# Holding four small products back until both of their loads are in, in a two-layer decoder trunk

## The chip, the cores and the metric

The kernel runs on one core of one Trainium2 chip. The metric is the device time of one execution in microseconds (us), as the median of several runs. All profiles are of that one core.

## The reference, cut to what matters

Two layers, each with two sub-layers, on 256 tokens of 1024 features. Six vectors of 1024 features per layer (shift, scale and gate of each sub-layer) come from one small vector `c` and a large matrix:

```python
c_act = jax.nn.silu(c)                                    # [1, 1024]
for l in range(DEPTH):                                    # 2
    ada = c_act @ w_ada[l] + b_ada[l]                     # [1, 1024] @ [1024, 6144]
    sh1, sc1, gt1, sh2, sc2, gt2 = split(ada, 6)
    u = x * (1.0 + sc1) + sh1
    y = mixer(u, ...)             # one wide projection; attention; convolution of 31 taps; two gates; output
    x = layer_norm(ALPHA * x + (1.0 + gt1) * y, ...)
    u = x * (1.0 + sc2) + sh2
    h = square(relu(u @ w_up[l])) @ w_down[l]
    x = layer_norm(ALPHA * x + (1.0 + gt2) * h, ...)
```

The change touches `sh2` and `sc2` of layer 0 alone: two thousand columns of `w_ada[0]`, each a dot product over 1024 features. They are needed when `u` of the second sub-layer is made.

## The kernel before, in words

All large weights stream through the core once, in units of 128 x 1024 (512 KB). `Stream.make` (lines 109 to 127) loads a unit on the queue of the SP engine (L118), copies its high part on ScalarE (`wh`, L121) and subtracts to get the low part on VectorE (`wl`, L122). Five raw tiles and eight split tiles are there, so up to eight units stand split ahead of the products. Each product is made of three matmuls of parts (L314 to L316 with 512 columns, L320 to L322 with 256).

Work that isn't weight products is traced in steps between the units by the class `Background`: the convolution (`conv_steps`, on VectorE and ScalarE), the attention (`attn_steps`), and the second shift and scale of layer 0, `ada_pe_cols(0, 4)` and then `ada_pe_cols(0, 3)`. A scheduler then orders each engine's instructions: among those that its own estimate of time calls ready, the one traced earliest goes first. After that every engine works through its own list strictly in that order, and so does the SP queue, which issues both the weight loads (L118) and the loads of `w_ada` (L379). A wait at the head of a list holds all that stands behind it.

Two thousand columns are four chunks of 512. For a chunk, `ada_pe_chunk` makes four loads of 256 x 512 (512 KB, two row blocks of 128 each) into tiles `ada`, of which there are three. After the second and after the fourth load, `ada_part` (L385) issues four products: each has a stationary operand of 32 columns (one of them with values) and writes its own 32 rows of one bank `adab`, side by side in the array (`tile_position=(0, 32 * j)`). Two of the four read the first load's tile and two the second's. After eight products ScalarE copies the bank (`adae`, L394), TensorE transposes it (`adat`, L368), and VectorE adds the four rows up (`adac`, L422, L423). So there are 16 loads and 8 groups of four products. A float32 product is two matmul records in the profile, so a group is 8 records and one half of it, a pair, is 4.

The first shift and scale go through the same `ada_part`, called from `ada_pe`, which the change leaves as it is (`adabs` in the profile).

Of the kernel before, what the change touches and what calls it, by code (L numbers as in the profile page):

```python
# [69 lines left out]
class Background:  # L70
    """Work that is traced a step at a time between the weight units; each step says after how many
    units the next one comes."""
# [18 lines left out]
    def finish(self, gen, until=None):  # L91
        """the rest of gen, or its steps until a condition holds"""
        for e in list(self.gens):
            if e[0] is gen and until is None:
                self.gens.remove(e)
        while until is None or not until():
            if next(gen, self) is self:
                break


class Stream:
    """The weights in the order of their use: each unit of [128, 1024] is loaded once and
    split exactly into a high and a low part, ahead of the products that take it."""
# [47 lines left out]
def trunk_kernel(ctx: ExitStack, tc: tile.TileContext, x_in, c_in, positions, w_in, w_attn_br,  # L151
                 conv_dw_w, conv_dw_b, conv_ln_g, conv_ln_b, w_conv_pw, w_out, w_ada, b_ada,
                 ln_mix_g, ln_mix_b, w_up, w_down, ln_ffn_g, ln_ffn_b, out):
    nc = tc.nc
# [48 lines left out]
    def load_ada0(k0, nk):  # L203
        """128 nk columns each of the first shift and scale"""
        src = w_ada[0, :, 0:2 * D].rearrange("(j p) (v n) -> p j v n", p=128, v=2)
        r = []
        for q in range(2):
            p, tag = (c_p, "c") if k0 % 2 else (g_p, "g")
            t = p.tile([128, 4, 2, 128 * nk], F32, name=f"ada0_{k0}{q}", tag=tag)
            for v in range(2):  # L210
                nc.sync.dma_start(t[:, :, v, :], src[:, 4 * q:4 * q + 4, v, 128 * k0:128 * (k0 + nk)])
                if small:
                    next(small[0], None)
            r.append(t)
        return r

    small = []
# [4 lines left out]
    rows, taps = [], []  # L222
    posi = const.tile([128, 2], I32, name="posi")

    def vector_loads(l):
        """per-feature vectors as rows, a load at a time"""
        r = t_p.tile([92, 128], F32, name=f"rows{l}", tag="t")
        rows.append(r)
        t = t_p.tile([4 * CK, 128], F32, name=f"taps{l}", tag="t")
        taps.append(t)  # L230
        o = 0
        for v, n in ((b_ada, 48), (ln_mix_g, 8), (ln_mix_b, 8), (ln_ffn_g, 8), (ln_ffn_b, 8),
                     (conv_ln_g, 4), (conv_ln_b, 4), (conv_dw_b, 4)):
            nc.sync.dma_start(r[o:o + n, :], v[l:l + 1, :].rearrange("o (j p) -> (o j) p", p=128))
            o += n
            yield
        nc.sync.dma_start(t, conv_dw_w[l].rearrange("j (q p) -> (j q) p", p=128))
        yield
        if l == 0:
            for h in range(2):  # L240
                nc.sync.dma_start(posi[:, h:h + 1], positions[0:1, H[h]].rearrange("o p -> p o"))
                yield
# [25 lines left out]
    units = []  # L268
# [35 lines left out]
    def order(later, earlier):  # L304
        """on the same engine, with no wait"""
        tc.add_manual_dep(later.ins, earlier.ins.name,
                          mybir.DependencyInfo(mybir.DependencyClass.NoSync, mybir.DependencyReason.DATA), reason="order")
# [4 lines left out]
    def rowmm(b, lh, ll, wh, wl, first, last):  # L312
        """b[tok, n] += lhs^T w, from the parts."""
        nc.tensor.matmul(b, lh, wh, start=first, stop=False, skip_group_check=True)  # L314
        nc.tensor.matmul(b, lh, wl, start=False, stop=False, skip_group_check=True)  # L315
        return nc.tensor.matmul(b, ll, wh, start=False, stop=last, skip_group_check=True)  # L316

    def colmm(b, wh, wl, rh, rl, first, last):
        """b[feat, tok] += w^T rhs, from the parts; two groups share a bank."""
        nc.tensor.matmul(b, wh, rh, start=first, stop=False, skip_group_check=True)  # L320
        nc.tensor.matmul(b, wh, rl, start=False, stop=False, skip_group_check=True)  # L321
        nc.tensor.matmul(b, wl, rh, start=False, stop=last, skip_group_check=True)  # L322

    def place(instrs, n):
        """instrs, of TensorE, after the next n products of a unit's half that are traced"""
        places.append([n, instrs])
# [21 lines left out]
    def col_group(ids, rhs, banks):  # L348
        """banks: two of [128, 2 feature tiles x 256]; units of [128, 2 kt, 512]."""
        for n, i in enumerate(ids):  # L350
            wh, wl = ws.live[i]
            for k in range(2):
                rh, rl = rhs(2 * n + k)
                first, last = n == 0 and k == 0, n == len(ids) - 1 and k == 1
                for f in range(4):
                    fs = slice(512 * k + 128 * f, 512 * k + 128 * f + 128)
                    o = banks[f // 2][:, 256 * (f % 2):256 * (f % 2) + 256]
                    if len(rh.shape) == 3:
                        o = o.rearrange("p (h t) -> p h t", h=2)
                    colmm(o, wh[:, fs], wl[:, fs], rh, rl, first and f % 2 == 0, last)  # L360
            ws.done(i)
            bg.step()

    def transpose4(src, name, made=None):
        """[128 tok, 512] -> bank [128 feat, 4, 128 tok]"""
        b = bank(name, tr)
        for i in range(4):
            t = nc.tensor.transpose(b[:, 128 * i:128 * i + 128], src[:, 128 * i:128 * i + 128], ident)  # L368
            if made is not None:
                made.append(t)  # L370
        return b

# [1 line left out]
    adac = [const.tile([128, 48], F32, name=f"adac{l}") for l in range(L)]  # L374

    def ada_load(l, v, c, q):
        n0 = v * D + 512 * c
        t = ada_p.tile([128, 2, 512], F32, name=f"ada{l}{v}{c}{q}", tag="ada")
        nc.sync.dma_start(t, w_ada[l, q * 256:(q + 1) * 256, n0:n0 + 512].rearrange("(j p) n -> p j n", p=128))  # L379
        return t  # L380

    def ada_part(b, srcs, first, last, after=None):
        """on TensorE, four features' rows side by side: partial sums in rows 0, 32, 64, 96"""
        for j, src in enumerate(srcs):
            m = nc.tensor.matmul(b[32 * j:32 * j + 32, :], cpad[:, (0 if first else 4) + j, :], src,  # L385
                       start=first, stop=last, tile_position=(0, 32 * j))
            if after is not None:
                order(m, after)
        return m
# [13 lines left out]
    def ada_pe_chunk(l, v, c):  # L403
        tiles = []
        for q in range(4):
# [4 lines left out]
            if q % 2:  # L410
                ada_part(b, [tiles[q - 1 + j // 2][:, j % 2] for j in range(4)], q == 1, q == 3)
# [20 lines left out]
    def gate_rows(t, c, sel, e):  # L432
        """1 + gate, the same in every row"""
# [20 lines left out]
    def ada_dve_cols(l, v):  # L454
        """shift v and scale v + 1 on VectorE: summed over the partitions at the end"""
# [24 lines left out]
    def ada_dve_gate(l, v, hold, before=None, gap=None):  # L480
        """the gate before this one has the tile until it is used"""
# [51 lines left out]
    def norm_half(h, banks, gt, gb=None):  # L533
        """x[h] <- normalised (alpha x + (1 + gate) y), with no gain and bias where they aren't given"""
# [34 lines left out]
    def gain_bias(l, v_sc, v_sh, g, b):  # L569
        """G = g (1 + sc), B = b (1 + sc) + sh, as columns"""  # L570
# [9 lines left out]
    def conv_steps(l, hold):  # L580
# [5 lines left out]
        # some taps' products come from ScalarE, two channel tiles at a time  # L586
# [45 lines left out]
    def attn_steps(l, qkT, vs, hold):  # L632
        # q comes with -1 / sqrt(HEAD_DIM): the scores are negated, their least is minus the maximum
# [91 lines left out]
    def glu_gate(h, c, a, g):  # L725
        """convolution channels 256 c .. of tokens 128 h .."""
# [9 lines left out]
    def first_proj(u):  # L736
        """Layer 0: the first columns of u as soon as the first shift and scale have come, and the
        products of the convolution's input and the queries with them."""
# [17 lines left out]
        def busy(n, after):  # L756
            """TensorE's clock rises with its work: products that nothing reads"""
# [33 lines left out]
        def first_mm(kk, w, q):  # L791
            """the products of feature tile kk, to be traced in parts"""
# [19 lines left out]
        def start(kk, after=None):  # L812
            """the columns of u for feature tile kk, then the split of the weights that meet them"""
# [33 lines left out]
    def mixer(l, u):  # L847
# [35 lines left out]
        else:  # L883
            # convolution branch's input with its gate
# [16 lines left out]
            # queries and keys  # L901
# [16 lines left out]
            # values  # L918
# [16 lines left out]
        # branch gates, as tanh(x / 2)  # L935
# [47 lines left out]
    def relu2_split(src, hh, hl, view):  # L983
        """hh + hl = relu(src)^2, split"""
# [75 lines left out]
    def vector_cols(l):  # L1060
        """per-feature vectors as columns"""
# [16 lines left out]
    def late_setup():  # L1078
# [38 lines left out]
    def last_rows(ids, lhs, banks):  # L1117
        """The last tokens' sums, columns one part after another, and the output from them."""
# [9 lines left out]
        # the last quarter's last sums have a bank of their own  # L1128
# [103 lines left out]
```

## Time and profile before

| | |
|---|---|
| time, median of 3 runs | 761.99 us (761.98 to 762.95) |
| span of the profiled execution | 760.8 us |
| TensorE (PE) busy | 740.3 us, 97% of the span |
| VectorE (DVE) busy | 593.4 us, 78% |
| ScalarE (ACT) busy | 448.9 us, 59% |
| granted TensorE clock, mean | 0.996 |

The profile covers the span from the first to the last instruction; the page gives no device time of its own for that execution, and the span lies 1.2 us under the median of the runs. PE is the matmul part of TensorE and PEld its weight loads, which overlap. An engine that is busy nearly all the time sets the end; idle time of the others costs nothing unless that engine waits for it.

### The profile page before, as it was taken

How to read it: one execution, taken by the hardware profiler on the slowest of the kernel's cores; microseconds unless marked ns; L12 is line 12 of the kernel's file. 1: busy time of each engine (PE TensorE's matmuls, PEld its weight loads, DVE VectorE, ACT ScalarE, POOL GpSimd, SP SyncE). 2: the span in 40 equal slices, each digit the busy share in tenths (PEclk: the TensorE clock that was granted, in tenths of full speed). 3: DMA queues.
4: the chain of work that ended last, by engine and by line, in shares of the span. 5: the costliest groups of instructions: out<-in, count | busy, mean ns of one | idle time of the engine just before them, and what ended most of it. 6: DMA issues, size and time to landing. Idle time of an engine off the chain costs nothing.

```text
span 760.8 us, 12246 instructions
## 1 busy us (share of the span) xinstructions
PE 740.3 (97%) x4648; PEld 633.5 (83%) x4648; DVE 593.4 (78%) x870; ACT 448.9 (59%) x737; POOL 15.1 (2%) x37
## 2 busy tenths in 40 slices
PE   6999999999999999999999999999999999999995
PEld 4667677999887999899877888899988889999995
DVE  3448987999889987788889899998869884454537
ACT  4449787975376645555545885876447565445530
POOL 0000000010000000000000000001000000000001
PEclk9999999999999999999999999999999999999998
DMA  9998869687386998899897645446546886666501
GB/s 286 309 334 325 318 217 314 205 263 222 130 301 223 360 402 330 301 332 356 253 314 254 222 149 162 136 137 216 178 157 232 289 306 191 203 183 184 188 1 55
DMA packets 81562, 181.40 MB, mean 238 GB/s; under 512 B 6264, under 2 KB 24544, under 8 KB 81504
## 3 DMA queue, kind: packets, MB, share of 16 engines
q1 hardware_dynamic: 81440, 180.61, 71.0%
q8 instruction: 36, 0.59, 0.3%
q14 instruction: 22, 0.18, 0.1%
q10 hardware_dynamic: 64, 0.02, 0.0%
HBM read 179.56 MB, written 1.05 MB: 237 GB/s over the span
## 4 chain that ended last, share of the span: by engine, by line
PE 77%; DVE 9%; DMA 5%; issue 3%; SPq 2%; ACT 2%; POOL 1%; POOLq 0%; DVEq 0%; ACTq 0%
PE d L314 7%; PE d L315 7%; PE d L316 7%; PE ua L320 3%; PE ub L321 3%; PE ub L320 3%; PE ua L322 3%; PE ub L322 3%; PE ua L321 3%; DMA ada<-in_w_ada_dram 3%; DVE wl L122 3%; DVE acc L600 2%; PE ga L320 2%; PE ga L321 2%; PE gb L320 2%
## 5 line engine op out<-in xcount | busy, mean ns | idle before, releaser
L121 ACT ACTIVATE wh<-w 128x1024 fp32r<-128x1024 f32 x232 | 244.8, 1060 | 191.6 <-PE ub L321 59.3
L122 DVE TENSOR_TENSOR wl<-w,wh 128x1024 fp32r<-128x1024 f32 x232 | 281.6, 1222 | 89.8 <-ACT wh L121 89.0
L314 PE MATMUL d<-wh,hh 128*128 128x512 f32 (+1 forms) x256 | 99.6, 389 | 0.0
L315 PE MATMUL d<-wl,hh 128*128 128x512 f32 (+1 forms) x256 | 98.9, 386 | 0.0
L316 PE MATMUL d<-wh,hl 128*128 128x512 f32 (+1 forms) x256 | 98.8, 386 | 0.0
L600 DVE SCALAR_TENSOR_TENSOR acc<-hconv,vc,acc 128x256 f32<-128x256 f32 x150 | 65.2, 486 | 0.0
L314 PEld LDWEIGHTS d<-wh,hh 128*128 128x128 f32 x256 | 48.1, 188 | 10.1 <-ACT relusq L988 0.8
L316 PEld LDWEIGHTS d<-wh,hl 128*128 128x128 f32 x256 | 48.1, 188 | 9.8
L315 PEld LDWEIGHTS d<-wl,hh 128*128 128x128 f32 x256 | 48.2, 188 | 9.1
L320 PE MATMUL ua<-uh,wh 128*128 128x256 f32 x192 | 54.5, 284 | 0.0
L322 PE MATMUL ua<-uh,wl 128*128 128x256 f32 x192 | 54.3, 283 | 0.0
L320 PE MATMUL ub<-uh,wh 128*128 128x256 f32 x192 | 54.3, 283 | 0.0
L321 PE MATMUL ub<-ul,wh 128*128 128x256 f32 x192 | 54.3, 283 | 0.0
L321 PE MATMUL ua<-ul,wh 128*128 128x256 f32 x192 | 54.3, 283 | 0.0
L322 PE MATMUL ub<-uh,wl 128*128 128x256 f32 x192 | 54.3, 283 | 0.0
L596 ACT ACTIVATE tap<-hconv,vc 128x256 f32<-128x256 f32 x90 | 39.3, 501 | 1.0 <-DVE qk L715 1.0
L491 DVE SCALAR_TENSOR_TENSOR adaa<-ada,ccol,adaa 128x1024 f32<-128x1024 f32 x28 | 35.8, 1279 | 3.9 <-DMA ada<-in_w_ada_dram 3.8
L320 PEld LDWEIGHTS ua<-uh,wh 128*128 128x128 f32 x192 | 36.8, 192 | 1.3 <-issue 0.8
L320 PE MATMUL ga<-uh,wh 128*128 128x256 f32 x128 | 37.7, 295 | 0.0
L321 PEld LDWEIGHTS ua<-ul,wh 128*128 128x128 f32 x192 | 36.8, 192 | 0.4
L320 PE MATMUL gb<-uh,wh 128*128 128x256 f32 x128 | 36.9, 288 | 0.0
L320 PEld LDWEIGHTS ub<-uh,wh 128*128 128x128 f32 x192 | 36.9, 192 | 0.0
(274 smaller groups left out, 1710.4 us busy)
## 6 DMA issues: line engine op xcount, KB each, us to landing
ada<-in_w_ada_dram SPq DMA_DIRECT2D x80, 512.0 KB, 5.3
w<-in_w_in_dram SPq DMA_DIRECT2D x72, 512.0 KB, 5.3
w<-in_w_up_dram SPq DMA_DIRECT2D x64, 512.0 KB, 5.0
w<-in_w_down_dram SPq DMA_DIRECT2D x64, 512.0 KB, 5.2
ada<-in_w_ada_dram SPq DMA_DIRECT2D x32, 256.0 KB, 6.0
w<-in_w_out_dram SPq DMA_DIRECT2D x16, 512.0 KB, 3.3
w<-in_w_attn_br_dram SPq DMA_DIRECT2D x8, 512.0 KB
w<-in_w_conv_pw_dram SPq DMA_DIRECT2D x8, 512.0 KB, 3.8
```

The costliest lines, as they stand in the source:

```text
L121: a = nc.scalar.activation(wh, w, AF.Copy)
L122: b = nc.vector.tensor_tensor(wl, w, wh.bitcast(F32), op=ALU.subtract)
L314: nc.tensor.matmul(b, lh, wh, start=first, stop=False, skip_group_check=True)
L315: nc.tensor.matmul(b, lh, wl, start=False, stop=False, skip_group_check=True)
L316: return nc.tensor.matmul(b, ll, wh, start=False, stop=last, skip_group_check=True)
L320: nc.tensor.matmul(b, wh, rh, start=first, stop=False, skip_group_check=True)
L321: nc.tensor.matmul(b, wh, rl, start=False, stop=False, skip_group_check=True)
L322: nc.tensor.matmul(b, wl, rh, start=False, stop=last, skip_group_check=True)
L491: nc.vector.scalar_tensor_tensor(acc, src, ccol[:, j:j + 1], acc, op0=ALU.mult, op1=ALU.add)
L596: nc.scalar.activation(p[:, q % 2, :], hconv[:, q, j:j + S], AF.Copy, scale=w(j, q))
L600: nc.vector.scalar_tensor_tensor(acc[:, q, :], hconv[:, q, j:j + S], w(j, q), acc[:, q, :], op0=ALU.mult, op1=ALU.add)
```

## The change

`ada_load` returns its DMA beside its tile, and `ada_part` takes a list of loads. In `ada_pe_chunk` each of the four products gets a real dependency, with a wait, on both loads of its group. Before, a product depended on the one load whose tile it reads. Everything else in the diff is comments.

```diff
     def ada_load(l, v, c, q):
         n0 = v * D + 512 * c
         t = ada_p.tile([128, 2, 512], F32, name=f"ada{l}{v}{c}{q}", tag="ada")
-        nc.sync.dma_start(t, w_ada[l, q * 256:(q + 1) * 256, n0:n0 + 512].rearrange("(j p) n -> p j n", p=128))
-        return t
+        return t, nc.sync.dma_start(t, w_ada[l, q * 256:(q + 1) * 256, n0:n0 + 512].rearrange("(j p) n -> p j n", p=128))

-    def ada_part(b, srcs, first, last, after=None):
+    def ada_part(b, srcs, first, last, after=None, loads=()):
         for j, src in enumerate(srcs):
             m = nc.tensor.matmul(b[32 * j:32 * j + 32, :], cpad[:, (0 if first else 4) + j, :], src,
                        start=first, stop=last, tile_position=(0, 32 * j))
             if after is not None:
                 order(m, after)
+            for d in loads:
+                tc.add_manual_dep(m.ins, d.ins.name,
+                                  mybir.DependencyInfo(mybir.DependencyClass.Sync, mybir.DependencyReason.DATA), reason="together")
         return m
...
             if q % 2:
-                ada_part(b, [tiles[q - 1 + j // 2][:, j % 2] for j in range(4)], q == 1, q == 3)
+                ada_part(b, [tiles[q - 1 + j // 2][0][:, j % 2] for j in range(4)], q == 1, q == 3,
+                         loads=[t[1] for t in tiles[q - 1:]])
```

## Rows read from the trace of the kernel before

**Rows 1.** The page's first part: busy us, share of the span, instructions.

```profile
PE 740.3 (97%) x4648; PEld 633.5 (83%) x4648; DVE 593.4 (78%) x870; ACT 448.9 (59%) x737; POOL 15.1 (2%) x37
```

**Rows 2.** Stages: length; busy us of PE, PEld, DVE, ACT, POOL; clock; DMA share, GB/s.

```profile
60.00:131.00 71.00, 70.03 (x424) 49.23 (x422) 62.67 (x136) 58.25 (x115) 0.34 (x8) 1.00 0.82 292
131.00:201.00 70.00, 69.97 (x533) 64.36 (x532) 62.71 (x103) 47.31 (x103) 2.07 (x2) 1.00 0.69 224
```

**Rows 3.** PE's waits, 60 to 210 us: total us, times, longest.

```profile
PE adab L385 <- DMA ada<-in_w_ada_dram: 1.0, 2, 0.8
```

**Rows 4.** The group of the changed products: least, median, longest ns; first, last start.

```profile
L385 PE MATMUL adab<-ada,cpad x64: 592/605/617, 70.4 to 130.5; 128*32 128x512 f32 x64
```

**Rows 5.** PE's timeline, key and value products: start, length, line, tile, count.

```profile
72.15 0.40 PE L315 MATMUL v<-wl,uh 128*128 128x512 f32 x1
72.48 1.05 PE L385 MATMUL adab<-ada,cpad 128*32 128x512 f32 x4
73.46 0.50 PE L316 MATMUL v<-wh,ul 128*128 128x512 f32 x1
73.80 0.40 PE L314 MATMUL k<-wh,uh 128*128 128x512 f32 x1
74.03 0.39 PE L315 MATMUL k<-wl,uh 128*128 128x512 f32 x1
...
76.62 1.05 PE L385 MATMUL adab<-ada,cpad 128*32 128x512 f32 x4
...
80.33 1.05 PE L385 MATMUL adab<-ada,cpad 128*32 128x512 f32 x4
```

**Rows 6.** PE's timeline, gate products: a group that stands together by itself.

```profile
122.87 0.28 PE L321 MATMUL gb<-ul,wh 128*128 128x256 f32 x1
122.99 0.28 PE L322 MATMUL gb<-uh,wl 128*128 128x256 f32 x1
123.19 1.06 PE L385 MATMUL adab<-ada,cpad 128*32 128x512 f32 x8
124.19 0.38 PE L320 MATMUL ga<-uh,wh 128*128 128x256 f32 x1
124.41 0.28 PE L321 MATMUL ga<-ul,wh 128*128 128x256 f32 x1
```

**Rows 7.** PE's timeline: the two groups whose second pair waits for its load.

```profile
110.30 1.05 PE L385 MATMUL adab<-ada,cpad 128*32 128x512 f32 x4
111.28 0.39 PE L320 MATMUL ga<-uh,wh 128*128 128x256 f32 x1
111.84 1.05 PE L385 MATMUL adab<-ada,cpad 128*32 128x512 f32 x4 [0.18 <-DMA ada<-in_w_ada_dram]
...
127.25 1.05 PE L385 MATMUL adab<-ada,cpad 128*32 128x512 f32 x4
...
129.99 1.05 PE L385 MATMUL adab<-ada,cpad 128*32 128x512 f32 x4 [0.79 <-DMA ada<-in_w_ada_dram]
```

**Rows 8.** The loads of line 379: us from issue to landing.

```profile
DMA to landing us min/median/max: 4.0/4.6/5.3
```

**Rows 9.** The chain that ended last: two loads on it, start and length.

```profile
107.83 3.97 DMA ada<-in_w_ada_dram
124.29 5.66 DMA ada<-in_w_ada_dram
```

**Rows 10.** SP's queue in order of time: one weight load.

```profile
108.29 0.42 SPq L118 DMA_DIRECT2D w<-in_w_in_dram  x1
```

**Rows 11.** SP's waits, 65 to 131 us.

```profile
SPq L379 <- PE adab L385: 33.5, 12, 9.4
```

**Rows 12.** VectorE's waits, 60 to 135 us.

```profile
DVE mx L656 <- PE s L651: 6.3, 3, 2.6
```

**Rows 13.** VectorE's timeline: a split, and the last low part before the output projection.

```profile
120.71 1.22 DVE L122 TENSOR_TENSOR wl<-w,wh 128x1024 fp32r<-128x1024 f32 x1
...
194.35 1.29 DVE L971 SCALAR_TENSOR_TENSOR ml<-gate,mh 128x512 fp32r<-128x512 f32 x2
```

## The prediction

> **What bounds the kernel now.** I read the page's busy times first, then the stages around the change, then the waits of TensorE, then its timeline instruction by instruction, and last the queues that could take a gain back. The page says TensorE: 740.3 of 760.8 us busy [rows 1]. In the stretch that the change touches and in the one behind it TensorE is busy 70.03 of 71 and 69.97 of 70 us at a granted clock of 1.00, that is 2.4 GHz throughout [rows 2]. VectorE stands next, at 62.7 us in each [rows 2]. From 60 to 210 us TensorE waits for a changed product's load only twice, 1.0 us in all [rows 3]. So in these stages time taken off TensorE's own list is time off the end, as long as VectorE and the loads keep up. The waits are not what there is to gain. What there is to gain is the time that the products themselves take.
>
> **What a pair costs.** The changed products are 64 records of 605 ns [rows 4], but they overlap, so the price must be read from the starts of their neighbours. Among key and value products one start follows the other by 0.23 us (73.80 to 74.03). Where a pair stands, the neighbours before and behind it start at 72.15 and 73.46, and the next one at 73.80 [rows 5]. Without the pair the third start would have been 72.15 + 2 x 0.23 = 72.61; the pair costs 73.80 - 72.61 = 1.19 us. Of this about 0.1 us lies ahead of it and 0.1 us behind it (0.33 us before its start and 0.34 us after its successor's, in place of 0.23).
>
> **What a whole group costs.** Two groups already stand together by chance: the records of one are eight in a row, started at 123.19 [rows 6]. The gate products' beat is 0.12 us (122.87 to 122.99). From 122.99 the second start behind the group is 124.41; without it that would have been 123.23, so a group of four products costs 1.18 us. Four cost what two cost. The array works on the four side by side, and a pair leaves half of it empty.
>
> The Trainium skill (TensorE: Matmul & The Clock Gate, Measured speedup vs the span model) states 2.38 times for three such column tiles, so three would last 1.26 of one. My estimate from that page is 1.13 for two and 1.39 for four, which would make the group about 0.2 us longer than the pair and the sum below about 5.7 in place of 7.0 us. The trace disagrees: 1.06 us for eight records, 1.05 for four [rows 5, 6], and the sum goes by the trace.
>
> **The sum on TensorE.** 64 records are 8 groups of 8. Two stand together (the one of rows 6, and one of the same form at 106.73), six are split in two pairs, which is twelve pairs. If the change joins the six, six pairs go: 6 x 1.17 = 7.0 us (1.17 being the mean of the two readings less a little for the one semaphore wait more that a group may need, which I set at 0.01 to 0.05 us). That is the whole gain that the edit can give. The number of products, loads and copies stays.
>
> **What the added wait costs.** A tile `ada` comes free when its products are done, and there are three tiles. Load 3 took its tile from the first pair of group 1; now it can only be issued after the whole of group 1, as can load 4. In general load 2k + 1 now follows group k, and group k + 1 waits for that load. Load, group, load, group become one chain. What hides a landing of 4.0 to 5.3 us, median 4.6 [rows 8], is the work on TensorE's list between two groups. Group 1's second pair ends about 73.5, group 2's second pair starts at 80.33 [rows 5]: 6.8 us between, less 1.2 for the pair at 76.62 that moves out, is 5.6 us. Groups 3 and 4 have nearly the same distance (5.4 and 5.6 by the same count); groups 5 and 7 have some 10 us. These five are covered by the median landing and by the longest, by little in three of them.
>
> The other two are those that wait already. Group 6 waits for a load issued at 107.83 that took 3.97 us, group 8 for one issued at 124.29 that took 5.66 [rows 9]. Their first pairs, at 110.30 and 127.25 [rows 7], stood in the shadow of that landing. With them gone TensorE arrives 1.2 us earlier and the load doesn't, so the waits of 0.18 and 0.79 us would become 1.4 and 2.0: 2.4 us more, if the places on the list stay. The other bound is nothing: the scheduler, by its own estimate, can put other ready products there, as the single gate product at 111.28 stands between the two pairs of group 6 [rows 7]. I take 1.4 us, a little over the middle, because only attention's work stands between 127.25 and 129.99 and group 8 has little else to draw on.
>
> **What is queued behind the waits.** On TensorE: the attention's and the gates' products, which every later stage takes from. On ScalarE: the copy of the bank, in order among the splits; it ends with the second load as before. On the SP queue: `w_ada`'s loads already hold that queue 33.5 us from 65 to 131 us, waiting for the products to free a tile [rows 11], and the weight loads stand behind. Odd loads will be issued later, at most by the distance of two pairs (3.7 us between 76.62 and 80.33). The weights bear this: the load issued at 108.29 [rows 10] is, by count, the 33rd unit, and its low part is written at 120.71 [rows 13], 12.4 us later, while the slower of the two loads of the same size on the chain took 5.66 us to land [rows 9]. I cost it at nothing; if that cover of some 6.7 us were gone, VectorE's splits would be late first, and TensorE only after the eight split units ahead are used up.
>
> **VectorE.** It has 63 us of work in each stage of 70 us [rows 2] and must follow. It can: 6.3 us of its idle time before 135 us is waiting for the attention's scores, three times [rows 12], and these scores come as much earlier as TensorE does. But that is the whole of its slack in this stage, and just ahead of the output projection the last low part of the merged branches ends at 195.64 (194.35 + 1.29) [rows 13], while the projection's second half needs it at about 195.5. A gain near 6 us is therefore what VectorE can pass on. I take 0.2 us lost here, with 0 and 1.5 as bounds.
>
> **The forecast.** 7.0 - 1.4 - 0.2 = 5.4 us. The profiled span of 760.8 us would be 755.4; the span stands 1.2 us below the median of the runs, 761.99, so the median would be 756.6 us. With every bound at its best it is 755.0, with every bound at its worst (2.4 us of waits, 0.05 x 8 of semaphores, 1.5 on VectorE) 759.3. Orders on all engines are worked out anew, which I allow 0.7 us more at the lower end: 754.3 to 759.3 is this case's own range.
>
> **Rivals.**
>
> (a) *The load chain makes TensorE wait: slower.* Its place is the wait at the head of the groups. If the scheduler puts a group where its first pair stood, the cover shrinks: group 2 would start 3.1 us after group 1's end (73.5 to 76.62), groups 3, 4, 6 and 8 have 4.7, 3.4, 2.5 and 3.0 us. At a landing of 5.66 us, the longest row, the waits are 2.6 + 1.0 + 2.3 + 3.2 + 2.7 = 11.8 us, of which 1.0 is paid already. 10.8 - 7.0 = 3.8 us slower: 765.8 us. It decides from an added wait of 1.4 us in each of these five groups on. For it: two waits exist before the change, and both at second pairs. Against it: all second pairs stood some way behind their landing, and the median landing is 4.6. At that the same places cost some 6 us and the change breaks even. Chance 0.09.
>
> (b) *VectorE takes it all: no change.* If VectorE's list before 195 us does not move, the projection waits for the last low part at 195.64 and the time stays at 762. For it: rows 13 and the 90% of busy time. Against it: its three waits for scores are TensorE's doing and go when TensorE is earlier. Chance 0.07.
>
> (c) *The products don't come together.* The dependencies make four products ready at once, but an instruction traced earlier could still go between them; then each pair costs what it did, and the time is 762 with the waits of (a) in small. Against it: the group at 123.19 shows four products that were ready at once and stayed together. Chance 0.06.
>
> **Range and chances.** The joined groups have 0.78. No run can tell less than 0.2%, 1.5 us, from no change here, since the three runs lie 1.0 us apart. Faster by more than that: 0.78. Within it: (b), (c) and the mild form of (a), 0.14. Slower: 0.08. The range runs from 754.3 to 761.5 us, which leaves out the slow form of (a), the upper half of no change, and a little at the bottom.
>
> **What the profile after will show if the steps are right.** The changed products still have 64 records, from 70 to about 125 us, in eight blocks of eight records of 1.0 to 1.1 us each. No block of four is left. TensorE's waits for `w_ada` at them grow from 1.0 us to about 2.4, at groups 6 and 8. VectorE's waits for scores before 135 us fall from 6.3 us to about 1 to 2. The third gate's first product comes some 5 us earlier, and the output projection too. If blocks of four remain, (c) was right; if TensorE's waits at the groups sum to more than 8 us, (a); if the groups are joined and the gates early but the projection starts where it did, (b). The prediction is wrong too if a reordered list costs more elsewhere than the 1.5 us allowed.

## The result, and the profile after

| | before | after |
|---|---|---|
| time, median | 762.10 us (760.65 to 763.30, 6 runs) | 755.82 us (752.48 to 759.66, 6 runs) |
| profiled execution: span, own time | 760.8 us, not given | 753.2 us, 755.1 us |

The ratio is 0.9917, 95% interval 0.9899 to 0.9935: 6.3 us faster, between 5.0 and 7.7. The forecast was 756.6 us. A second set of runs of the same kernel beside the experiments gave 0.9908 (0.9891 to 0.9925).

The page's first part after, which answers to [rows 1]:

```profile
PE 733.7 (97%) x4648; PEld 633.3 (84%) x4648; DVE 592.7 (79%) x870; ACT 448.5 (60%) x737; POOL 15.0 (2%) x37
```

TensorE has the same 4648 records and 6.6 us less busy time. The changed products in the chain that ended last, from 60 to 140 us (start, length, engine, tile, line, count), answer to the pairs of [rows 5, 7]:

```profile
73.44 1.00 PE adab L385 x8
79.88 1.00 PE adab L385 x8
86.58 0.99 PE adab L385 x8
93.22 1.00 PE adab L385 x8
103.30 1.02 PE adab L385 x8
104.32 3.89 DMA ada<-in_w_ada_dram
108.35 1.06 PE adab L385 x8
118.82 1.00 PE adab L385 x8
124.07 0.99 PE adab L385 x8
```

Eight blocks of eight records and no block of four. One of them with its neighbours, in TensorE's timeline:

```profile
79.27 0.39 PE L314 MATMUL k<-wh,uh 128*128 128x512 f32 x1
79.49 0.39 PE L315 MATMUL k<-wl,uh 128*128 128x512 f32 x1
79.81 1.06 PE L385 MATMUL adab<-ada,cpad 128*32 128x512 f32 x8
80.81 0.50 PE L316 MATMUL k<-wh,ul 128*128 128x512 f32 x1
81.14 0.39 PE L314 MATMUL v<-wh,uh 128*128 128x512 f32 x1
```

At the beat of 0.23 us the last start would have been 79.49 + 0.46 = 79.95 without the group: it costs 1.19 us, as one pair did [rows 5]. The second semaphore costs nothing that shows.

The waits of TensorE (60 to 210 us) and of VectorE (60 to 135 us), and the landing of line 379's loads, answer to [rows 3, 12, 8]:

```profile
PE adab L385 <- DMA ada<-in_w_ada_dram: 0.4, 1, 0.4
```

```profile
DVE mx L660 <- PE s L655: 0.4, 2, 0.2
```

```profile
DMA to landing us min/median/max: 3.8/3.8/3.9
```

The added wait did not come in this execution: 0.4 us in place of 1.0, where the forecast had 2.4. VectorE's waiting for scores went from 6.3 to 0.4 us; it followed TensorE all the way.

The landing line needs care, and so does [rows 8]: it covers only two of the 16 loads, before as well as after, which are those whose end the profile can match to their issue. The chain of before has a load of 5.66 us [rows 9], above the "max" of [rows 8]. From one issue to the last of its 16 semaphore updates in the trace, all 16 loads took 4.0 to 7.3 us before (median 5.4) and 3.8 to 7.5 us after (median 5.5). The landings did not become shorter.

VectorE's last low part before the output projection, which answers to [rows 13], ends at 187.57 + 1.29 = 188.86 in place of 195.64:

```profile
187.57 1.29 DVE L975 SCALAR_TENSOR_TENSOR ml<-gate,mh 128x512 fp32r<-128x512 f32 x2
```

To say where the time went, one length serves for all kernels here: from the first key product (`k`) to the first product of the MLP (`u`), both on line 314. The stage of the change lies inside, the first projection ahead of it is left out, and so is all that follows. Before and after, by the first of the two times in each row (first and last start):

```profile
L314 PE MATMUL u<-wh,uh x32: 389/389/477, 213.9 to 236.9; 128*128 128x512 f32 x32
L314 PE MATMUL k<-wh,uh x16: 388/393/499, 60.5 to 90.0; 128*128 128x512 f32 x16
```

```profile
L314 PE MATMUL u<-wh,uh x32: 389/389/477, 207.1 to 230.1; 128*128 128x512 f32 x32
L314 PE MATMUL k<-wh,uh x16: 389/389/499, 61.7 to 87.5; 128*128 128x512 f32 x16
```

That is 153.4 us before and 145.4 after, 8.0 us less. The first projection, ahead of this length, took 1.2 us more in this execution, in code that is the same. Its stages after (length; busy us of PE, PEld, DVE, ACT, POOL; clock; DMA share, GB/s) show the granted clock of TensorE near its lower level, 1.2 of 2.4 GHz, for a part of it:

```profile
14.00:16.00 2.00, 2.00 (x15) 0.87 (x17) 0.19 (x1) 0.00 (x0) 0.00 (x0) 0.51 1.05 367
16.00:18.00 2.00, 2.00 (x15) 0.98 (x6) 0.00 (x0) 1.07 (x2) 0.00 (x0) 0.64 1.17 309
```

Before, the clock is 1.00 in both of these stretches, and in after_again too. In the 4 us ahead of them TensorE was busy 2.0 us here, 2.4 before and 4.0 in after_again. The clock lost, 0.49 and 0.36 of 2 us each, is enough to cover the 1.2 us.

### The profile page after: what moved, and what is told of

Its sections match the earlier page's. It is cut to its first block, busy times and chain, and to the rows that moved or that the text cites. A ratio compares the mean times of both kernels' runs of the same rounds, so it can differ in the third digit from the quotient of the medians.

```text
span 753.2 us, 12252 instructions
## 1 busy us (share of the span) xinstructions
PE 733.7 (97%) x4648; PEld 633.3 (84%) x4648; DVE 592.7 (79%) x870; ACT 448.5 (60%) x737; POOL 15.0 (2%) x37
## 3 DMA queue, kind: packets, MB, share of 16 engines
HBM read 179.56 MB, written 1.05 MB: 240 GB/s over the span
## 4 chain that ended last, share of the span: by engine, by line
PE 84%; DMA 6%; DVE 4%; ACT 2%; issue 2%; SPq 1%; POOL 1%; POOLq 0%; DVEq 0%; ACTq 0%
PE d L315 6%; PE d L316 6%; PE d L314 6%; DMA ada<-in_w_ada_dram 4%; PE ua L320 3%; PE ua L322 3%; PE ua L321 3%; PE ub L321 3%; PE ub L320 3%; PE ub L322 3%; PE ga L320 2%; PE gb L320 2%; PE ga L321 2%; PE gb L321 2%; PE ga L322 2%; PE gb L322 2%
```

## The experiments

Ratios are to the kernel before, run beside them; five rounds each. "Stage" is the length from `k` to `u` in the profiled execution, and "waits" is how long TensorE waited in it at the changed products (`adab`).

| kernel | median us | ratio (95% interval) | stage us | waits us |
|---|---|---|---|---|
| before | 763.6, 763.1, 763.8 | 1 | 153.4 | 1.0 |
| after_again | 756.83 | 0.9908 (0.9891 to 0.9925) | 147.1 | 2.0 |
| v4_joined | 759.35 | 0.9940 (0.9922 to 0.9958) | 148.8 | 1.0 |
| v3_joined | 761.22 | 0.9975 (0.9961 to 0.9990) | 151.4 | 1.6 |
| pairs_apart | 756.14 | 0.9904 (0.9888 to 0.9920) | 146.7 | 0.3 |
| zero_between | 766.69 | 1.0049 (1.0034 to 1.0064) | 156.4 | 0 |
| zero_behind | 759.24 | 0.9953 (0.9939 to 0.9967) | 149.0 | 0.4 |
| one_column | 777.32 | 1.0194 (1.0178 to 1.0211) | 167.4 | 0 |
| gap12 | 759.10 | 0.9949 (0.9936 to 0.9962) | 148.7 | 0 |
| raw4 | 765.19 | 1.0017 (0.9994 to 1.0040) | 147.0 | 1.9 |
| raw4_bufs4 | 761.99 | 0.9986 (0.9966 to 1.0006) | 147.3 | 1.4 |
| raw4_eight | 762.12 | 0.9977 (0.9957 to 0.9996) | 146.5 | 1.6 (no cause named) |

The first profiled execution of the changed kernel had a stage of 145.4 us and waits of 0.4.

The theory: a place on TensorE's list costs some 1.18 us, whether it holds two products or four. The main rival: the gain comes from what the wait brings with it, later loads, other orders, fewer waits.

**after_again**, the changed kernel once more.

> The changed kernel once more, as the reference for the kernels beside it. All theories: some 756 us, 0.992 of the kernel before.

As expected. Its profiled execution waited longer at groups 6 and 8 than the first one, in TensorE's timeline:

```profile
107.41 1.07 PE L385 MATMUL adab<-ada,cpad 128*32 128x512 f32 x8 [0.69 <-DMA ada<-in_w_ada_dram]
...
124.43 1.06 PE L385 MATMUL adab<-ada,cpad 128*32 128x512 f32 x8 [1.29 <-DMA ada<-in_w_ada_dram]
```

2.0 us here and 0.4 us there, in the same code: these waits differ from one execution to the next, and the stage with them (147.1 and 145.4 us). Less the waits the two stages are equal, 145.1 and 145.0 us, and that of before is 152.4.

**v4_joined and v3_joined**, one half of the change each.

```diff
-                         loads=[t[1] for t in tiles[q - 1:]])
+                         loads=[t[1] for t in tiles[q - 1:]] if v == 4 else ())      # v == 3 in the other
```

> Only the second scale has the new waits: groups 1 to 4, all of which were split in pairs. Theory: 4 pairs go, 4 x 1.17 = 4.7 us, some 757.4 us (ratio 0.994). Rival (the gain is the two waits for a load, groups 6 and 8, 1.0 us and what follows from them): no gain here, 762 us.

> Only the second shift has the new waits: groups 5 to 8, of which two were split in pairs. Theory: 2 pairs go, 2 x 1.17 = 2.3 us, and up to 0.6 us of waits: some 759.4 us (ratio 0.9965). Rival (the gain is the two waits for a load): all of the gain is here, some 756 us.

Four pairs gone gave 0.60%, 4.6 us (1.15 a pair); two gone gave 0.25%, 1.9 us (0.95 a pair); six in the whole change 0.83 to 0.92%, 6.3 to 7.0 us (1.05 to 1.17). The gain goes with the count of pairs, and so do the stages less their waits: 4.6 us shorter than before for four pairs, 2.6 for two, 7.3 to 7.4 for six. The half that holds the waits for loads has the smaller share, and in it they did not go: 1.6 us at two groups in place of 1.0. TensorE's waits, 60 to 210 us, of v3_joined:

```profile
PE adab L385 <- DMA ada<-in_w_ada_dram: 1.6, 2, 1.3
```

**pairs_apart**: both waits kept, the second pair ordered behind the next weight product that is traced.

```diff
+    def part_pairs(m):                    # called with the last matmul of every weight product
+        for t in held:
+            order(t, m)
+        held.clear()
...
+            if loads and j >= 2:
+                held.append(m)
```

> Both waits are kept on all four products, but the second pair of a group is ordered behind one weight product, so that 8 groups are 16 pairs again. Theory (a place on TensorE's list costs 1.18 us, whether it holds two products or four): 8 x 1.17 = 9.4 us more than the changed kernel, some 765 us, about 2 to 3 us slower than the kernel before, which had only 14 places. Rival (the gain comes from the later loads and the new order that the wait brings, not from the products): stays at some 756 us.

A miss, for a reason that the chain that ended last shows. Only the last two groups came apart; ahead of the first six the next product traced had already gone by the time the loads were in.

```profile
102.34 1.02 PE adab L395 x8
103.36 3.82 DMA ada<-in_w_ada_dram
107.32 1.06 PE adab L395 x8
117.80 0.98 PE adab L395 x4
119.33 0.98 PE adab L395 x4
124.21 0.98 PE adab L395 x4
125.93 0.98 PE adab L395 x4
```

For two groups the theory has 2.3 us, and the time shows none: the ratio is that of after_again. Less the waits, the stage is 146.4 us, some 1.4 us longer than in either execution of the changed kernel. The waits hid that: group 8 did not wait here, since group 7's second pair stood in the landing of its load, and in after_again it waited 1.29 us. The remaining 0.9 us of the 2.3 is open. This run does not tell the theories apart, and the next pair of kernels was made for it.

**zero_between and zero_behind**: a small product of zeros, added to the bank, ordered between the two pairs of all eight groups or behind all four products.

```diff
+    def zero_product(b, ms, loads):       # waits for both loads, ordered behind the products ms
+        z = nc.tensor.matmul(b[0:64, 0:CK - 1], cpad[:, 0:2, :].rearrange("p k n -> p (k n)"), hconv[:, 0, 0:CK - 1],
+                             start=False, stop=False, skip_group_check=True)
...
+            if loads and j == 2:          # zero_between; zero_behind: after the loop over j
+                z = zero_product(b, ms, loads)
```

> The changed kernel with one small product of zeros (64 rows, 30 columns, added to the same bank) ordered between the first and the second pair of all 8 groups, so that they cannot overlap, at the same place on TensorE's list. Theory (four side by side last as long as two): each group costs one more place, 8 x 1.1 to 1.2 us plus the zero products, 9 to 11 us more than the changed kernel: 766 to 768 us, 3 to 5 us slower than the kernel before, which had 14 places and not 16. Rival (the gain is order and waiting): within 1 to 2 us of the changed kernel, 757 to 758 us.

> The same 8 zero products behind the four products of each group in place of between them: the control. Theory: only the zero products themselves, 8 x 0.1 to 0.3 us, 757 to 759 us. If the zero products and not the parting are what costs in the kernel beside it, this one is as slow as that.

TensorE's timeline at group 1, first zero_between, then zero_behind:

```profile
71.61 0.39 PE L316 MATMUL k<-wh,ul 128*128 128x512 f32 x1
71.92 1.05 PE L388 MATMUL adab<-ada,cpad 128*32 128x512 f32 x4
72.91 0.30 PE L401 MATMUL adab<-hconv,cpad 128*64 128x30 f32 x2
73.14 1.05 PE L388 MATMUL adab<-ada,cpad 128*32 128x512 f32 x4
74.12 0.50 PE L314 MATMUL v<-wh,uh 128*128 128x512 f32 x1
```

```profile
71.86 0.39 PE L316 MATMUL k<-wh,ul 128*128 128x512 f32 x1
72.19 1.07 PE L386 MATMUL adab<-ada,cpad 128*32 128x512 f32 x8
73.18 0.30 PE L399 MATMUL adab<-hconv,cpad 128*64 128x30 f32 x2
73.41 0.50 PE L314 MATMUL v<-wh,uh 128*128 128x512 f32 x1
```

From the first changed product to the next weight product it is 2.20 us with the pairs apart and 1.22 with them together: 0.98 us for one more pair, with the same instructions, dependencies and loads. Eight times that is 7.8 us; the medians differ by 766.69 - 759.24 = 7.45, the stages by 7.4. The control waited 0.4 us for a load and zero_between did not, which is what parts 7.4 from 7.8. The control itself stands 3.4 us over the changed kernel by the ratios; eight zero products at 0.23 us are 1.8 of it, and the rest was not followed up.

**one_column**: the four products of a group accumulate in the same 32 rows, so they cannot run side by side.

```diff
-            m = nc.tensor.matmul(b[32 * j:32 * j + 32, :], ..., tile_position=(0, 32 * j))
+            i = 0 if loads else j
+            m = nc.tensor.matmul(b[32 * i:32 * i + 32, :], ..., tile_position=(0, 32 * i), ...)
```

> All four products of a group write the same 32 rows, the first quarter of the array's columns, and accumulate there; they still stand together and wait for both loads. The copy of the bank takes 32 rows, and the transposes and the sum are shorter. Theory (the gain is the overlap of different column quarters): four products one after the other, 8 records of some 0.43 us, 3.4 us and some 0.2 us at the ends in place of 1.18: 8 x 2.4 = 19 us more, some 775 us. Rival (the gain is that TensorE changes between the forms of product 8 times and not 14): stays at some 756 us.

In the chain that ended last a group is now 3.55 us (the first of eight, all alike):

```profile
72.04 3.55 PE adab L386 x8
```

8 x (3.55 - 1.00) = 20.4 us; the ratios give 0.0286, 21.8 us, the stages 20.3 to 22.0. So the four products gain little from standing together as such; they gain from four different quarters of the array's columns (and of the bank's rows, which go with them; no run parts the two). A product took 3.55 / 4 = 0.89 us here, so by this estimate at most some 0.3 of the 1.18 us of a place are the change from one form of product to another.

**gap12**: the steps between the loads further apart.

```diff
-ADA_GAP = 0.8
+ADA_GAP = 1.2
```

> The changed kernel with the steps between the loads set from 0.8 to 1.2 units, so that more weight products stand between an issue and the group that needs it. If the waits at the groups are a cost of 0.4 to 2.0 us in the changed kernel, they go, and the time is 0 to 1.5 us below it: some 755.5 us. If the later end of the chunks delays what needs them, it is slower than the changed kernel.

A miss: TensorE has no wait for these loads any more in the profile, and yet the time is 0.41% above after_again, 3.1 us. Three things show in TensorE's timeline. The fourth group came apart again, with attention's work in its middle:

```profile
100.55 1.05 PE L385 MATMUL adab<-ada,cpad 128*32 128x512 f32 x2
101.52 0.70 PE L652 MATMUL s<-kT,qT 64*128 64x256 f32 x4
...
102.48 1.06 PE L385 MATMUL adab<-ada,cpad 128*32 128x512 f32 x6
103.47 0.38 PE L320 MATMUL ga<-uh,wh 128*128 128x256 f32 x1
```

Then, where the convolution's end is due, TensorE waits for VectorE twice:

```profile
157.71 0.63 PE L368 MATMUL cbk<-ident,cn 128*128 128x128 f32 x4 [0.51 <-DVE cn L621]
163.37 0.66 PE L697 MATMUL av<-PT,vs 128*64 128x256 f32 x4 [0.58 <-DVE cn L621]
```

And at the first product of the MLP, the end of the stage, for ScalarE:

```profile
210.27 0.50 PE L314 MATMUL u<-wh,uh 128*128 128x512 f32 x1 [0.61 <-ACT uh L527]
```

That is 1.2 + 1.1 + 0.6 = 2.9 us. Less the waits for loads, the stage is 148.7 us, 3.6 longer than after_again's; the remaining 0.7 us was not settled.

The parted group tells one thing more. Its one product (two records) took 0.97 us to the start of the next, its three (six records) 102.48 to 103.47, 0.99. With two at 0.98 and four at 1.00, a place costs the same from one product to four.

**raw4, raw4_bufs4 and raw4_eight**: a fourth tile for `w_ada`, for which one of the five raw weight tiles had to go, and all eight products of a chunk together.

```diff
-RAW = 5
+RAW = 4                      # all three
-ADA_BUFS = 3
+ADA_BUFS = 4                 # raw4_bufs4 and raw4_eight
...
+        for q in (1, 3):     # raw4_eight: after the fourth load, each product waits for all four
+            ada_part(b, [tiles[q - 1 + j // 2][0][:, j % 2] for j in range(4)], q == 1, q == 3,
+                     loads=[t[1] for t in tiles])
```

> The changed kernel with four raw weight tiles in place of five, which makes room for a fourth tile of w_ada: the control for the two kernels beside it. Weight loads run one unit less ahead of the splits; eight units stand split ahead of TensorE, so at most 1 us slower than the changed kernel, some 757 us.

> Four raw weight tiles and four tiles of w_ada: the second load of the next group no longer waits for this group's products, so the chain load, group, load, group is cut. If that chain costs what TensorE's waits at groups 6 and 8 showed (0.4 us in one execution, 2.0 in another), the waits are gone and the time is 0.4 to 2 us below the kernel with four raw tiles alone. If the chain is hidden, the two are equal.

> As the one beside it with four tiles of w_ada, but all eight products of a chunk wait for its four loads and stand together: 4 places on TensorE's list in place of 8, each of two rounds of four (2 x 0.98 us) and one pair of ends (0.2 us). By the reading that 0.2 us of a place lies at its ends, 4 x 0.2 = 0.8 us below raw4_bufs4; the later last load of a chunk can take that back. If it beats all others, it is the version to keep.

The control was a miss by 7 us: without the fifth raw tile the whole gain is gone. It is not lost in this stage (147.0 us, as after_again) but behind it: from `u` to the last product of the last MLP raw4 takes 543.7 us and after_again 536.5. From 206 us on TensorE waits 7.9 us in raw4 and 2.9 in after_again, and from 400 to 480 us the granted clock is 0.98 in raw4 and 1.00 there; the two cover most of the difference.

The fourth tile of `w_ada` gives 0.31% back, 2.4 us, with intervals that overlap, and not here either (147.3 us). Groups 6 and 8, which waited 0.6 us in raw4, no longer wait, as the cut chain would have it, but group 1 does. TensorE's waits, 60 to 210 us, and the group in TensorE's timeline, of raw4_bufs4:

```profile
PE adab L385 <- DMA ada<-in_w_ada_dram: 1.4, 1, 1.4
```

```profile
73.50 1.07 PE L385 MATMUL adab<-ada,cpad 128*32 128x512 f32 x8 [1.43 <-DMA ada<-in_w_ada_dram]
```

Group 1 waits in raw4 as well, 1.28 us, so this wait seems to come with the raw tile that went, not with the `w_ada` tile that came. The loads land a little later with four tiles, 6.6 us in the median of all 16 against 5.9 in raw4. The granted clock parts these kernels' runs: the five of raw4_bufs4 at 0.997 or more took 760.6 to 761.2 us, the seven at 0.988 to 0.994 took 761.3 to 766.5.

Eight together make the stage 0.8 us shorter than the kernel beside it, as expected in the stage, and the medians equal. No version here beats the changed kernel beyond the intervals.

## Why the prediction was right

**What bounds the kernel.** Right. In this stretch TensorE's list sets the end: it has 6.6 us less busy time (5.2 in after_again), and the time is 6.3 to 7.0 us less, at the same instructions.

**The price of a pair and of a group.** Right, and shown four ways. The group with its neighbours costs 1.19 us, as a pair did. Halves of the change gain in the ratio of the pairs that go. Parting all eight groups by a product of zeros costs 0.98 us a group on the list and 7.45 us in all against its control. Taking away the side by side, and nothing else of the order, costs 20 us. The prediction's estimate from the Trainium skill (TensorE: Matmul & The Clock Gate, Measured speedup vs the span model), 2.38 times for three column tiles, had four tiles last some 0.2 us longer than two. The span model of that section, some 4 ns for each further tile, has them nearly equal, and the trace agrees with that: eight records took 1.00 us and four 0.98, while the same eight in one column quarter took 3.55.

**The sum of 7.0 us.** Right in size: the stage less its waits is 7.3 to 7.4 us shorter. In all it was 6.3 and 7.0 us in the two sets of runs, where 5.4 was forecast after the losses.

**The added wait, 1.4 us.** Mis-sized in the first execution, near in the second. The waits went from 1.0 to 0.4 us there (0.6 less) and to 2.0 in after_again (1.0 more). The places on the list moved in part, as the forecast's middle way assumed. Had they stayed, group 6 would have stood 2.7 us of work behind group 5's end (107.83 to 111.84 [rows 7, 9], less the wait of 0.18 and a pair of 1.17), and group 8 3.7 behind group 7's by the same count; they stand 3.6 and 4.2 behind, in both executions. What differs between the two is the landing. Group 8's last load took 5.66 us before [rows 9] and 5.38 in after_again, where the group waited 1.29 us; in the first execution it was issued at 119.84, and the group started at 124.00 without a wait, so it had landed within 4.2. The forecast read its landing of "4.0 to 5.3, median 4.6" from [rows 8], which are two of 16 loads. For the loads that its argument turns on, the last of groups 2 to 8, the trace of before has 4.0 to 5.8 us with a median of 4.7; that the two came so near was luck.

**The load chain as a rival (a), slower.** Wrong in size: the waits never reached 3 us in all. With the chain cut by a fourth tile the waits at groups 6 and 8, 0.6 us in raw4, were gone, and the stage did not become shorter.

**VectorE, 0.2 us, and rival (b).** Right that it can follow: its 6.3 us of waiting for scores turned into 0.4 (1.6 in after_again; 1 to 2 was foreseen), and its last low part came 6.8 us earlier. No run measures the 0.2 by itself.

**Rival (c), the products don't come together.** Wrong for this change, where all eight groups stood together. But gap12 shows that it can be: two dependencies make four products ready at once, and do not bind them.

**The span and the time.** The forecast set the profiled execution 1.2 us under its own time; after it was 1.9 us (753.2 and 755.1), as in the runs of before beside the experiments (763.71 us and 761.8, for one), so that the span of before is likely that of an execution near 762.7. It changes nothing in the difference.

## What to carry to other kernels

Small products that use different column quarters of the array cost one place on TensorE's list together, and one place more each time that something gets between them. Where TensorE is the bound, count the places, read the price of one from the starts of its neighbours, and hold early products back until their partners are ready. Then look at what the wait delays; here the later loads were for the most part hidden by other work, and changing the pace or the buffers to remove the rest cost more than it gave.

## What was not expected of the hardware

Loads of 512 KB on the same queue took from 4.0 to 7.3 us within one execution, and one and the same load 5.66 us before [rows 9], 5.38 in after_again and at most 4.2 in the first execution after. A single product of 32 columns took as long as four side by side, 0.97 us against 1.00. Four products in one column quarter took 3.55 us against 1.00 in four quarters, a factor of 3.55 out of 4. A product of 30 columns in another form between two pairs took only 0.23 us.
